# A decoder layer in fp32 on one core: other places for the matmuls that are issued as 64 and 192 columns

## The chip, the core and the metric

The kernel runs on one core of one Trainium2 chip, in one launch. The metric is the time of that core in device microseconds. All arithmetic is fp32; a matmul's operands are declared as fp32r.

## What is computed

One layer of a decoder trunk, batch 1, 256 tokens, model width 2048, cut here to its matrix products:

```python
n = rmsnorm(h, g_mix);  z = n @ w_in                  # 2048 -> 5120: q, k, v, u
a = moba_attention(q, k, v, dist_bias)                # 8 heads of 128, one block of 256 keys: causal
c = conformer_conv(u, conv_w, ...)                    # gated, 31 taps per channel, layernorm, silu
h = h + concat([a, c]) @ w_out                        # 2048 -> 2048
h = h + cross_attention(rmsnorm(h, g_cross), rmsnorm(mem, g_mem), wq, wk, wv, wo)   # 4 heads, 256 memory tokens
nm = rmsnorm(h, g_mlp)
h = h + square(relu(nm @ w1)) @ w2                    # 2048 -> 8192 -> 2048
return rmsnorm(h, g_final)
```

## The kernel before

**Steps.** The host lays all weights out as 200 chunks of 128 x 2048 elements (1 MB each), in the order of their use. The kernel is one straight program of 200 steps, step j for chunk j: u is steps 0 to 15 (U0), v 16 to 23 (V0), q and k 24 to 39 (QK0), the memory's k and v 40 to 47, w_out 48 to 63 (WOUT0), cross attention's wq and wo 64 to 71, and the MLP 72 to 199 (MLP0). The MLP has four rounds of 32 steps: 16 for a quarter of w1 (72 to 87, 104 to 119, 136 to 151, 168 to 183), then 16 for the same quarter of w2.

**Products.** The kernel splits each operand into a high part, rounded to fp32r, and a low part, the rest, and makes a product of three matmuls: high x high, high x low, low x high. SP loads chunk j into a `raw` tile (4 buffers), ACT rounds it to `wh` (`split_high`), DVE takes the difference `wl` (`split_low`; between steps 8 and 47 POOL does this for every seventh chunk); `wh` and `wl` have 3 buffers each and are made two steps ahead. Activations stand as `act`, `mixa`, `mixc` or `s` tiles, their high and low parts side by side.

**Two kinds of step.** In `weight_stationary` (u, q and k, the memory's k, w_out, w1) a 128 x 128 block of weights is loaded into TensorE and 256 columns of activations stream through it: 16 blocks of weights times three, so 48 products of 256 columns. In `act_stationary` (v, the memory's v, w2) activations are loaded and 512 columns of weights stream: 24 products of 512 columns. Each matmul has a weight load of its own, also where two matmuls in a row have the same weights. The number of a product in its step, 0 to 47, is called its place here: `3 * (4 * i + m) + n`, with i the slice of 128 rows of the chunk, m the block of 128 columns, and n which of the three (0 high x high, 1 high x low, 2 low x high).

**Issued in two.** The table `PARTED` (line 43) names steps and places; `weight_stationary` issues a product that stands in it as two matmuls on the same weights, the first of 64 columns, the second of the other 192:

```python
if 3 * (nf * i + m) + n in PARTED.get(j, ()):
    mm(bk, o[:, 0:64], a, b[:, 0:64], False)
    mm(bk, o[:, 64:], a, b[:, 64:], stop)
else:
    mm(bk, o, a, b, stop)
```

**What stands between the products.** The order of each engine's work is written out by hand: `at(place, j, fn, frac)` hangs work on a step (early, pre, late, mid, post), and mid hooks run between the units of a step, a unit being the 12 products of one i. On TensorE they are short: the sums for a norm (`totals`, in steps 5, 15, 48, 76, and after 64), its spread over the partitions (`spread`, two transposes, in steps 6, 16, 49, 77), the scores, transposes and values of self-attention (after step 28, in 30, in 31, and so on every four steps), cross attention in 65 to 71, and transposes of h inside some w2 steps. All else in a `weight_stationary` stretch is products of 256 columns, one after the other. DVE also has the 31 taps of the convolution, spread over steps 7 to 46 (`fill`).

Of the kernel before, what the change touches and what calls it, by code (L numbers as in the profile page):

```python
# [38 lines left out]
WOUT_ORDER = [(0, 0), (1, 0), (2, 0), (0, 1), (1, 1), (2, 1), (3, 0), (3, 1)]  # L39
STEP_US = 5.25  # L40


PARTED = {2: (3, 7, 11), 6: (24, 28, 32), 24: (3, 7, 11), 50: (3, 7, 11), 77: (24, 28, 32),
          104: (3, 7, 11), 136: (3, 7, 11), 168: (3, 7, 11)}
WARM = 14

ROOM = 128
# [35 lines left out]
def tile_hybrid_block(ctx: ExitStack, tc: tile.TileContext, xT, memT, w, par, rel, gfin, out):  # L83
# [21 lines left out]
    def mm(bk, o, lhsT, rhs, stop):  # L105
        pe.matmul(o, lhsT=lhsT, rhs=rhs, start=not bk.begun, stop=stop, skip_group_check=True)  # L106
        bk.begun = True
# [192 lines left out]
    def weight_stationary(j, banks, kg, acts, kts=4, cols=512, last=None):  # L300
        units = []
        nf = cols // P
        for i in range(kts):
            def unit(i=i):
                for m in range(nf):
# [5 lines left out]
                    for n, (a, b) in enumerate(((h, hi), (h, lo), (l, hi))):  # L311
                        stop = last and i == kts - 1 and n == 2
                        if 3 * (nf * i + m) + n in PARTED.get(j, ()):
                            mm(bk, o[:, 0:64], a, b[:, 0:64], False)
# [764 lines left out]
```

## Time and profile before

| | |
|---|---|
| runs of the kernel before | 1159.45 us median, 1157.51 to 1162.56, 3 runs |
| the profiled execution, its own time | 1160.12 us |
| its span, first to last instruction | 1158.3 us |
| TensorE clock granted over the span | 0.997 of full speed |
| matmuls in the program | 7978 |

The profile names engines PE (matmuls), PEld (weight loads, which run beside matmuls), DVE, ACT, POOL and SP. A row of the timeline has a start in us from the span's start, a length, and how many instructions in a row it merges (x). The length of a matmul's record is longer than the distance to the next start, since matmuls are pipelined; so paces are read here from starts, not from lengths. The trace holds starts to 1 ns, the views print them to 10 ns.

### The profile page before, as it was taken

Reading aid. Unit: us, or ns where it says so; the run is one execution under the profiler, and the core shown is the slowest. Engines: PE = TensorE matmul, PEld = TensorE weight load, DVE = VectorE, ACT = ScalarE, POOL = GpSimd, SP = SyncE. Lnnn points to the kernel's source line nnn. Section 1 sums busy time; section 2 is a strip of 40 time slices with the busy share of each in tenths; the row PEclk is TensorE's granted clock in tenths of the full one; section 3 lists DMA queues with packets and bytes.
Section 4 is the critical chain, followed back from the end, with each engine's and each line's share of the span. In section 5 each row is a group of like instructions: output and inputs, shape, how many; then the busy total and the mean of one; then the engine's idle time right before and its main releaser. Section 6 shows DMA issues by size and latency. Waiting matters only on the chain.

```text
span 1158.3 us, 18581 instructions
## 1 busy us (share of the span) xinstructions
PE 1144.4 (99%) x8038; PEld 1069.5 (92%) x8038; DVE 705.5 (61%) x821; ACT 540.3 (47%) x565; POOL 123.2 (11%) x104
## 2 busy tenths in 40 slices
PE   8999999999999999999999999999999999999997
PEld 8998899998999999998889998889999889999886
DVE  6699997878666768545444454554545554455443
ACT  7654335474655556444333444333454333444342
POOL 2282022102004003000000200000000000000112
PEclk9999999999999999999999999999999999999999
DMA  9874744455455535455555645555544555554541
GB/s 349 287 219 170 272 184 173 154 182 182 169 190 192 179 134 194 155 227 192 191 182 182 218 158 211 208 187 184 184 178 185 215 184 195 193 190 149 218 145 73
DMA packets 35289, 221.04 MB, mean 191 GB/s; under 512 B 3848, under 2 KB 7304, under 8 KB 9736
## 3 DMA queue, kind: packets, MB, share of 16 engines
q1 hardware_dynamic: 33024, 216.98, 51.7%
q10 hardware_dynamic: 2184, 2.88, 1.2%
q8 instruction: 63, 1.03, 0.4%
q14 instruction: 18, 0.15, 0.0%
HBM read 216.18 MB, written 3.67 MB: 190 GB/s over the span
## 4 chain that ended last, share of the span: by engine, by line
PE 92%; DVE 4%; ACT 1%; DMA 1%; issue 1%; ACTq 0%; POOL 0%; DVEq 0%
PE mm L106 86%; PE cv L106 3%; DVE cv L72 2%; DVE wl L72 2%; PE sm L106 2%; DMA raw<-in_w_dram 1%; ACT wh L172 0%; DMA hT<-in_xT_dram 0%; PE sm L840 0%; PE sm L525 0%; DVE small L72 0%; PE sm L715 0%; DVE ring L72 0%; ACT act L200 0%; POOL hp L420 0%
## 5 line engine op out<-in xcount | busy, mean ns | idle before, releaser
L72 DVE TENSOR_TENSOR wl<-raw,wh 128x2048 fp32r<-128x2048 f32 (+1 forms) x205 | 444.5, 2175 | 296.8 <-ACT wh L172 291.8
L172 ACT ACTIVATE wh<-raw 128x2048 fp32r<-128x2048 f32 x195 | 373.7, 1916 | 501.8 <-PE mm L106 448.2
L106 PE MATMUL mm<-act,wh 128*128 128x256 f32 (+1 forms) x3214 | 566.0, 280 | 1.3 <-ACT wh L358 1.3
L106 PEld LDWEIGHTS mm<-act,wh 128*128 128x128 f32 x3214 | 490.0, 188 | 2.2 <-ACT wh L358 1.6
L106 PE MATMUL mm<-act,wl 128*128 128x256 f32 x1607 | 447.0, 279 | 0.4 <-DVE wl L72 0.4
L106 PE MATMUL mm<-wh,s 128*128 128x512 f32 (+1 forms) x1040 | 319.1, 387 | 0.0
L106 PEld LDWEIGHTS mm<-act,wl 128*128 128x128 f32 x1607 | 301.2, 188 | 1.0 <-DVE wl L72 1.0
L106 PEld LDWEIGHTS mm<-wh,s 128*128 128x128 f32 x1040 | 194.3, 188 | 39.2
L106 PE MATMUL mm<-wl,s 128*128 128x512 f32 (+1 forms) x520 | 200.7, 386 | 0.0
L106 PEld LDWEIGHTS mm<-wl,s 128*128 128x128 f32 x520 | 97.7, 188 | 19.4
L72 DVE SCALAR_TENSOR_TENSOR cv<-hp,part,cv 128x256 f32<-128x256 f32 x240 | 97.6, 478 | 0.0
L72 DVE TENSOR_TENSOR s<-ring,s 128x512 fp32r<-128x512 f32 x32 | 22.2, 692 | 66.6 <-ACT s L828 66.6
L944 POOL TENSOR_TENSOR acc<-acc,gb 128x512 f32<-128x512 f32 x6 | 11.9, 2010 | 458.1 <-ACT ring L860 458.1
L106 PE MATMUL mm<-wh,act 128*128 128x512 f32 x192 | 60.1, 391 | 0.0
L225 POOL TENSOR_TENSOR acc<-acc,ring 128x512 f32<-128x512 f32 x17 | 39.9, 2344 | 147.0 <-ACT ring L224 146.3
L106 PE MATMUL mm<-mixa,wh 128*128 128x256 f32 (+1 forms) x258 | 45.6, 280 | 0.0
L106 PEld LDWEIGHTS mm<-wh,act 128*128 128x128 f32 x192 | 36.0, 188 | 7.4
L182 POOL TENSOR_TENSOR wl<-raw,wh 128x512 fp32r<-128x512 f32 x24 | 32.5, 1386 | 95.4 <-ACT wh L172 95.4
L106 PEld LDWEIGHTS mm<-mixa,wh 128*128 128x128 f32 x258 | 39.3, 188 | 0.2
L106 PE MATMUL mm<-wl,act 128*128 128x512 f32 x96 | 37.4, 389 | 0.0
L106 PE MATMUL mm<-mixa,wl 128*128 128x256 f32 (+1 forms) x129 | 35.7, 278 | 0.0
L106 PE MATMUL mm<-mixc,wh 128*128 128x256 f32 x192 | 32.7, 276 | 0.0
(141 smaller groups left out, 745.2 us busy)
## 6 DMA issues: line engine op xcount, KB each, us to landing
raw<-in_w_dram SPq DMA_DIRECT2D x199, 1024.0 KB, 4.8
mem<-in_memT_dram SPq DMA_DIRECT2D x4, 512.0 KB, 8.4
hT<-in_xT_dram SPq DMA_DIRECT2D x3, 512.0 KB, 8.5
dram_rev<-rev ACTq DMA_DIRECT2D x1, 1532.0 KB
raw<-in_w_dram SPq DMA_DIRECT2D x4, 256.0 KB, 5.7
bias<-dram_rev SPq DMA_DIRECT2D x1, 1024.0 KB, 8.2
gb<-in_gfin_dram SPq DMA_DIRECT2D x4, 256.0 KB, 7.4
out_dram<-acc SPq DMA_DIRECT2D x4, 256.0 KB, 2.7
```

Source lines behind the costliest of these rows:

```text
L72: return op(out, *args, **kw)
L106: pe.matmul(o, lhsT=lhsT, rhs=rhs, start=not bk.begun, stop=stop, skip_group_check=True)
L172: act.activation(wh[j], raw[j], AF.Copy)
L182: pool.tensor_sub(wl[j][:, s], raw[j][:, s], wh[j].bitcast(F32)[:, s])
L225: eng.tensor_tensor(self.acc, self.acc, sq, op=OP.add)
L944: pool.tensor_mul(d, d, gb[cb])
```

## The change

Only the table changes. Before, eight steps had three products each that were issued in two: at places 3, 7 and 11, or at 24, 28 and 32. Now nine steps have them: steps 2 and 72 three each, the other seven one each. That makes 13 in place of 24, so 11 matmuls fewer in the program. Step 72 is new in the table; step 2 is the first u stretch's, 72 is the first step of the MLP.

```diff
-PARTED = {2: (3, 7, 11), 6: (24, 28, 32), 24: (3, 7, 11), 50: (3, 7, 11), 77: (24, 28, 32),
-          104: (3, 7, 11), 136: (3, 7, 11), 168: (3, 7, 11)}
+PARTED = {2: (5, 20, 36), 6: (24,), 24: (5,), 50: (3,), 72: (6, 21, 37), 77: (24,), 104: (6,), 136: (6,), 168: (6,)}
```

The order of all other instructions, on PE and on the other engines, is the same; names below differ in running numbers alone, and lines by the two that the table got shorter.

On PE at the start of step 104 (an MLP stretch; steps 136 and 168 read alike), before: `wh104` and `wl104` are the high and low part of chunk 104, `act0` the activations, `mm` a PSUM bank.

```order
L106 MATMUL mm_275_6373<-act0_213_4730,wh104_6301 128x256 x2
L106 MATMUL mm_275_6373<-act0_213_4730,wl104_6302 128x256
L106 MATMUL mm_275_6373<-act0_213_4730,wh104_6301 128x64
L106 MATMUL mm_275_6373<-act0_213_4730,wh104_6301 128x192
L106 MATMUL mm_275_6373<-act0_213_4730,wh104_6301 128x256
L106 MATMUL mm_275_6373<-act0_213_4730,wl104_6302 128x256
L106 MATMUL mm_276_6374<-act0_213_4730,wh104_6301 128x256
L106 MATMUL mm_276_6374<-act0_213_4730,wh104_6301 128x64
```

And now, from the same point:

```order
L104 MATMUL mm_275_6368<-act0_213_4724,wh104_6296 128x256 x2
L104 MATMUL mm_275_6368<-act0_213_4724,wl104_6297 128x256
L104 MATMUL mm_275_6368<-act0_213_4724,wh104_6296 128x256 x2
L104 MATMUL mm_275_6368<-act0_213_4724,wl104_6297 128x256
L104 MATMUL mm_276_6369<-act0_213_4724,wh104_6296 128x64
L104 MATMUL mm_276_6369<-act0_213_4724,wh104_6296 128x192
L104 MATMUL mm_276_6369<-act0_213_4724,wh104_6296 128x256
L104 MATMUL mm_276_6369<-act0_213_4724,wl104_6297 128x256
```

The pair of 64 and 192 columns has moved from the fourth product (place 3) to the seventh (place 6, the first of the next block of weights), and the pairs at places 7 and 11 are gone.

On PE at the start of step 24 (the first of q and k), before:

```order
L106 MATMUL mm_56_1636<-act0_2_118,wh24_1533 128x256 x2
L106 MATMUL mm_56_1636<-act0_2_118,wl24_1534 128x256
L106 MATMUL mm_56_1636<-act0_2_118,wh24_1533 128x64
L106 MATMUL mm_56_1636<-act0_2_118,wh24_1533 128x192
L106 MATMUL mm_56_1636<-act0_2_118,wh24_1533 128x256
L106 MATMUL mm_56_1636<-act0_2_118,wl24_1534 128x256
L106 MATMUL mm_57_1637<-act0_2_118,wh24_1533 128x256
L106 MATMUL mm_57_1637<-act0_2_118,wh24_1533 128x64
```

And now:

```order
L104 MATMUL mm_56_1634<-act0_2_118,wh24_1531 128x256 x2
L104 MATMUL mm_56_1634<-act0_2_118,wl24_1532 128x256
L104 MATMUL mm_56_1634<-act0_2_118,wh24_1531 128x256 x2
L104 MATMUL mm_56_1634<-act0_2_118,wl24_1532 128x64
L104 MATMUL mm_56_1634<-act0_2_118,wl24_1532 128x192
L104 MATMUL mm_57_1635<-act0_2_118,wh24_1531 128x256 x2
L104 MATMUL mm_57_1635<-act0_2_118,wl24_1532 128x256
L104 MATMUL mm_57_1635<-act0_2_118,wh24_1531 128x256 x2
```

The pair stands at place 5, on the low weights, in place of 3, 7 and 11.

## Rows read from the trace of the kernel before

**Rows 1.** the page, part 1: busy us (share of the span), instructions of each engine.
```profile
PE 1144.4 (99%) x8038; PEld 1069.5 (92%) x8038; DVE 705.5 (61%) x821; ACT 540.3 (47%) x565; POOL 123.2 (11%) x104
```

**Rows 2.** what PE waited for, whole span: us in total, times, longest us.
```profile
PE sm L257 <- DVE rr L72: 1.9, 1, 1.9
```

**Rows 3.** sums by stretch of 20 us: busy time and matmuls touched (x), granted clock.
```profile
60.00:80.00 20.00, 20.00 (x179) 1.00 0.76 208
151.00:171.00 20.00, 20.00 (x173) 1.00 0.68 263
480.00:500.00 20.00, 20.00 (x179) 1.00 0.67 247
640.00:660.00 20.00, 20.00 (x172) 1.00 0.67 238
```

**Rows 4.** timeline of PE, first products of steps 78, 88, 104, 105, 120, 136 (start, length).
```profile
470.52 0.39 PE L106 MATMUL mm<-act,wh 128*128 128x256 f32 x2
...
524.92 0.39 PE L106 MATMUL mm<-wh,s 128*128 128x512 f32 x1
...
615.91 0.40 PE L106 MATMUL mm<-act,wh 128*128 128x256 f32 x2
...
621.88 0.28 PE L106 MATMUL mm<-act,wh 128*128 128x256 f32 x1
...
706.68 0.39 PE L106 MATMUL mm<-wh,s 128*128 128x512 f32 x1
...
793.75 0.40 PE L106 MATMUL mm<-act,wh 128*128 128x256 f32 x2
```

**Rows 5.** timeline of PE, step 50: first and third split product, and what follows each.
```profile
304.83 0.50 PE L106 MATMUL mm<-mixa,wh 128*128 128x64 f32 x3
305.17 0.28 PE L106 MATMUL mm<-mixa,wl 128*128 128x256 f32 x1
...
305.96 0.36 PE L106 MATMUL mm<-mixa,wl 128*128 128x64 f32 x2
...
306.42 0.28 PE L106 MATMUL mm<-mixa,wl 128*128 128x256 f32 x1
```

**Rows 6.** timeline of PE, first split product of steps 2, 6, 24 and 77.
```profile
20.43 0.50 PE L106 MATMUL mm<-act,wh 128*128 128x64 f32 x3
20.77 0.28 PE L106 MATMUL mm<-act,wl 128*128 128x256 f32 x1
...
46.52 0.50 PE L106 MATMUL mm<-act,wh 128*128 128x64 f32 x3
...
145.34 0.50 PE L106 MATMUL mm<-act,wh 128*128 128x64 f32 x3
145.68 0.28 PE L106 MATMUL mm<-act,wl 128*128 128x256 f32 x1
...
467.46 0.50 PE L106 MATMUL mm<-act,wh 128*128 128x64 f32 x3
```

**Rows 7.** timeline of PE, step 104: its fourth product is the first split one.
```profile
616.15 0.28 PE L106 MATMUL mm<-act,wl 128*128 128x256 f32 x1
616.27 0.50 PE L106 MATMUL mm<-act,wh 128*128 128x64 f32 x3
```

**Rows 8.** timeline of PE, first products of steps 29, 33, 37 and 41.
```profile
174.69 0.47 PE L106 MATMUL mm<-act,wh 128*128 128x256 f32 x1
...
200.58 0.47 PE L106 MATMUL mm<-act,wh 128*128 128x256 f32 x1
...
225.84 0.47 PE L106 MATMUL mm<-act,wh 128*128 128x256 f32 x1
...
251.10 0.47 PE L106 MATMUL mm<-act,wh 128*128 128x256 f32 x1
```

**Rows 9.** timeline of PE (step 16) and of DVE (step 8): a wait in each.
```profile
103.90 0.43 PE L257 MATMUL sm<-ident,rr 128*128 128x128 f32 x2 [1.88 <-DVE rr L72]
...
54.17 0.49 DVE L72 TENSOR_SCALAR cv<-hp,part 128x256 f32<-128x256 f32 x1 [5.14 <-POOL hp L420]
```

## The prediction

> **What bounds the kernel now.** I read the page first: PE is busy 99% of the span [rows 1]. Then what PE waited for: its longest wait is one of 1.9 us for DVE [rows 2]. So the end is set by how closely PE's own products follow each other, and a busy PE does not tell that. The third view is the sums by stretch. All four stretches run products of 256 columns at the granted clock 1.00 (2.4 GHz), but 20 us touch 179 of them in two stretches and 172 or 173 in the other two [rows 3]. First starts of steps give the paces: the 480 products of steps 78 to 87 take 524.92 - 470.52 = 54.40 us, 113.33 ns each (the **tight** pace); the 720 of steps 105 to 119 take 706.68 - 621.88 = 84.80 us, 117.78 ns each (the **wide** pace) [rows 4]. A step of 48 is 5.440 us tight and 5.653 us wide, 0.213 us apart, 4.44 ns a product. The 384 products of 512 columns in steps 120 to 135 take 793.75 - 706.68 = 87.07 us, 226.7 ns each, twice the tight pace; only products of 256 columns can gain. The wide pace holds in the three MLP stretches from 104, 136 and 168 (16 steps each), 24 to 32, 2 to 6, 70 to 77, and pieces behind pauses.
>
> **What decides the pace.** The two kinds of stretch have the same instructions, so something that lasts from product to product differs. Three products on the tight pace take 340.0 ns, which is 51 units of 6.667 ns (16 columns at 2.4 GHz); three on the wide one 353.3 ns, which is 53 units. I took starts in ns (the rows print 10 ns), averaged like products of a stretch, and read them against a grid of 6.667 ns, with a drift of 2 ns per ms taken out, to some 0.6 ns. In all the tight stretches of 256 columns the products begin at one and the same offset, also behind pauses; I call it 0. On the wide pace the products go round in threes, at offsets 1.7, 5.8 and 3.3 ns. So the two paces are two locks against a grid that outlasts pauses, and a split product knocks PE out of one. Where it then lands follows from the offset at which it begins. First splits of a step: in 6, 50 and 77 (at 46.52, 304.83 and 467.46) the offset is 1.7 ns, and the tight pace begins within two products, before the second split. In 2 and 24 (at 20.43 and 145.34) it is 5.8 ns, and the pace stays wide [rows 5, 6]. In 104, 136 and 168 it is 2 ns, but the round has not settled: the product ahead took 120 ns (616.27 - 616.15) [rows 7], and the pace stays wide. Second and third splits in those five steps begin from what the earlier ones left and tell nothing of a settled round.
>
> **The change part by part.** *Splits.* A split on the tight pace adds one tight product: from 305.96 to 306.42 three products, one of them split, take 0.46 us where three take 0.34 (113 ns in ns starts) [rows 5]. The winning one from the wide round takes with the product behind it 305.17 - 304.83 = 0.34 us (338 ns) in place of 0.236 [rows 5]; a losing one adds about 0.105 us (145.68 - 145.34 = 0.34) [rows 6]. The change has 11 fewer.
>
> *Places.* Which of the three products of a block is split does not matter in the trace: settled splits at 5.8 ns do the same on high x high as on low x high. Going on by threes: in step 24 place 3 is at 5.8 ns, 4 at 3.3, so the new place 5 is at 1.7; step 2 is alike. Step 72 stands in a settled wide round with place 0, and so 3 and 6, at 1.7. In 104, 136 and 168 place 3 is at about 2 ns behind the 120 ns product. Where a 120 ns product stands elsewhere (behind first or second splits in steps 2, 24, 104, 136, 168) the next takes 117 or 118 and begins the round; by that place 4 is at 5.8, 5 at 3.3 and 6 at 1.7. So all new places hit the winning offset. Steps 6 and 77 are entered otherwise than before, on the tight pace up to the norm's sums in 5 and 76. From the tight pace those sums left place 0 at 1.7 in steps 15 and 65, which is what step 77 had before; so place 24 wins in both as it did. Step 50 is untouched upstream.
>
> *The sum, against the run's own 1160.12 us.*
> MLP, each of three: before 706.68 - 615.91 = 90.77 us [rows 4]; after 6 wide products (0.71), the pair and its neighbour (0.338) and 760 at the tight pace (86.13), 87.18. 3 x 3.59 = **10.77**.
> Steps 24 to 32: step 24 had 48 wide products and three losing splits, 5.97; after 5 x 0.1178 + 0.338 + 41 x 0.1133 = 5.57: 0.40. Steps 25 to 28: 4 x 0.213 = 0.85. Steps 29 to 32 become like 37 to 40, which are entered tight: 200.58 - 174.69 = 25.89 us against 251.10 - 225.84 = 25.26 [rows 8]: 0.63. Together **1.88**.
> Steps 2 to 6: step 2 keeps three splits, two of them now on the tight pace: 5.97 to 5.80, 0.17; steps 3 and 4 0.43; step 5 up to its sums 36 x 4.44 ns = 0.16; step 6 loses two splits, 0.24. Together **1.00**. Step 16 takes some back: PE waits there 1.88 us for DVE [rows 9]. That DVE work goes back without a gap that matters to its wait at 54.17 for the first convolution input [rows 9], which stands behind step 6's spread. It moves by what is won ahead of that, 0.76, and the other 0.24 makes the wait longer: **-0.24**. Bounds: 0 if DVE keeps up, -1.00 if it does not move.
> Step 50: two splits fewer, **0.23**. Steps 72 to 77: step 72 gets three splits, -0.15; 73 to 75 0.64; 76 up to its sums 0.11; 77 two splits fewer, 0.23: **0.82**.
> Sum 14.46 us. PE's supply stands it: steps 7 to 14 and 78 to 87 run tight with no wait of PE. That gives 1145.7 by the run shown, which is 0.7 us over the median 1159.45: **1145.0 us**.
>
> **The rivals.** *1. The MLP places miss.* They are the one place where the round has to settle from products that no row shows without a split. If place 6 is not at 1.7 ns there, all three stay wide, since they are entered alike: 10.77 goes, two losing splits less each return 0.63, **1155.1**. For it: another entry of the kind "wide after a pause" (step 6, behind its spread) takes longer to settle than I assume here. Against: the five 120 ns products that can be read all went on into the round at once.
> *2. One smaller stretch misses.* Step 24 alone: 1.67 us, **1146.7**; step 77 or 50, which have no second try any more: 2.2 and 3.2, up to **1148.2**; one MLP stretch of three, 1148.4.
> *3. The place decides nothing.* The operands' addresses or the history set the pace, and only the splits saved count: 11 x 0.106 = 1.2, **1158.3**. The Trainium skill speaks for this kind of view ("TensorE: Matmul & The Clock Gate", "Step-by-step: what each phase is for"): weight loads and the streaming operand have separate read ports, and "Loading the next tile's weights doesn't steal SBUF read bandwidth from the running matmul", by which there should be one pace and no offset that matters. The trace does not agree: it has two paces at one clock [rows 3], and three times the pace changes behind a split.
> *4. Slower.* The single splits in 6, 50 and 77 lose, where three tries stood before, because the offset at a place is not carried over as I read it. Then 6 to 15, 50 to 64 and 77 to 87 turn wide: 432, 717 and 504 products x 4.44 ns = 7.3 us; with all new places missing too and 1.2 saved, **1165.6**. It decides as soon as two of the three old winners lose and no MLP stretch wins; one that wins (3.6) hides it. For it: before, runs differ by 5 us, about one MLP stretch and more, so offsets may differ between runs; the first steps wait for loads. Against: stretches 24, 104, 136 and 168 begin behind long rows of 512 columns that wait for nothing.
>
> **How the numbers follow.** Forecast 0.70 (1143 to 1147), rival 1 0.13, rival 2 0.09, rival 3 0.04, rival 4 0.04. A measurement of this kernel tells about 0.5% from no change, 5.8 us: faster is below 1153.7. Forecast and rival 2 are faster, 0.79; rivals 1 and 3 no change, 0.17; rival 4 slower, 0.04. The range reaches from 1142.5 (step 16 gives nothing back, and what runs differ by) to 1150 (one stretch misses and step 16 takes all back); it leaves out rivals 1, 3 and 4.
>
> **What would show it.** In the sums by stretch of the changed kernel 20 us anywhere in 105 to 119, 25 to 28 and 73 to 75 should touch 179 products, not 172. The stretch from step 104 to 120 should be 87.2 us long, and 29 to 33 25.3. PE's wait in step 16 should be 2.1 us. If the pace changes at a place whose offset is not 1.7 ns, or does not where it is, the grid is wrong; if the paces come as said and the time does not, the wait list has a new line.

## The result, and the profile after

The changed kernel takes 1146.78 us (median of 4 runs, 1145.39 to 1148.68) against 1160.03 us (median of 4 runs, 1157.51 to 1162.56): a ratio of 0.989 with a 95% interval of 0.987 to 0.991, so 1.1% faster and clear of no change. The forecast was 1145.0 us, between 1142.5 and 1150.0, faster with 0.79. Profile against profile the span went from 1158.3 to 1143.8 us, 14.5 us, where the sum had 14.46. That agreement is better than the reasons deserve: the big term came as worked out, and among the small ones 1.7 us were missed and 1.8 us came unforeseen (the table further below).

The page's part 1 of the kernel after (busy us, share of the span, instructions), to set beside [rows 1]:

```profile
span 1143.8 us, 18559 instructions
PE 1130.8 (99%) x8027; PEld 1056.0 (92%) x8027; DVE 705.6 (62%) x821; ACT 540.4 (47%) x565; POOL 127.3 (11%) x104
```

PE is as busy as it was, 99%. The share says nothing of the gain; busy time and span fell together. The sums by stretch of 20 us, to set beside [rows 3] (start:end, busy time and matmuls touched of PE, PEld, DVE, ACT, POOL, then granted clock, DMA share, GB/s):

```profile
60.00:80.00 20.00, 20.00 (x179) 20.00 (x178) 19.19 (x33) 11.04 (x12) 17.92 (x11) 1.00 0.75 216
151.00:171.00 20.00, 20.00 (x179) 20.00 (x178) 20.00 (x32) 6.34 (x4) 1.97 (x2) 1.00 0.69 263
480.00:500.00 20.00, 20.00 (x178) 20.00 (x178) 11.66 (x8) 8.04 (x8) 0.00 (x0) 1.00 0.58 207
640.00:660.00 20.00, 20.00 (x179) 20.00 (x178) 11.40 (x8) 8.40 (x6) 7.03 (x4) 1.00 0.76 264
```

151:171 and 640:660 had 173 and 172 products, now 179, at the same granted clock 1.00. These are steps 25 to 28 and 109 to 112. The timeline of PE, first products of steps 78, 88, 104, the split of 104 and the product behind it, and the first products of 105, 120 and 136, to set beside [rows 4, 7]:

```profile
466.80 0.39 PE L104 MATMUL mm<-act,wh 128*128 128x256 f32 x2
...
521.20 0.39 PE L104 MATMUL mm<-wh,s 128*128 128x512 f32 x1
...
612.21 0.40 PE L104 MATMUL mm<-act,wh 128*128 128x256 f32 x2
...
612.92 0.50 PE L104 MATMUL mm<-act,wh 128*128 128x64 f32 x3
613.26 0.28 PE L104 MATMUL mm<-act,wl 128*128 128x256 f32 x1
613.37 0.28 PE L104 MATMUL mm<-act,wh 128*128 128x256 f32 x1
...
617.79 0.28 PE L104 MATMUL mm<-act,wh 128*128 128x256 f32 x1
...
699.39 0.39 PE L104 MATMUL mm<-wh,s 128*128 128x512 f32 x1
...
786.46 0.28 PE L104 MATMUL mm<-act,wh 128*128 128x256 f32 x1
```

Steps 104 to 119 take 699.39 - 612.21 = 87.18 us, where they took 90.77, and 87.18 was the forecast. The pair and the product behind it take 613.26 - 612.92 = 0.34 us, the next start follows after 0.11 us (613.37): the tight pace from there on. Steps 105 to 119 are 699.39 - 617.79 = 81.60 us, 113.33 ns a product. 136 and 168 are equal to it.

The small stretches did not all come as said. PE in step 2, its first product, the first split, the third split with the product behind it, and the first product of step 3, to set beside [rows 6]:

```profile
20.02 0.40 PE L104 MATMUL mm<-act,wh 128*128 128x256 f32 x2
...
20.60 0.36 PE L104 MATMUL mm<-act,wl 128*128 128x64 f32 x2
...
24.47 0.50 PE L104 MATMUL mm<-act,wh 128*128 128x64 f32 x3
24.81 0.28 PE L104 MATMUL mm<-act,wl 128*128 128x256 f32 x1
...
25.99 0.28 PE L104 MATMUL mm<-act,wh 128*128 128x256 f32 x1
```

Step 2 took 25.99 - 20.02 = 5.97 us, as before: three losing splits, and steps 3 and 4 stayed at 5.653 us. The first products of steps 29, 33, 37 and 41, to set beside [rows 8]:

```profile
172.41 0.47 PE L104 MATMUL mm<-act,wh 128*128 128x256 f32 x1
...
197.98 0.58 PE L104 MATMUL mm<-act,wh 128*128 128x256 f32 x2
...
223.56 0.59 PE L104 MATMUL mm<-act,wh 128*128 128x256 f32 x2
...
249.13 0.47 PE L104 MATMUL mm<-act,wh 128*128 128x256 f32 x1
```

29 to 33 take 25.57 us (25.89 before, 25.26 forecast), and 33 to 41 take 51.15 where they took 50.52: steps 35 to 38 had been partly tight and are wide now.

What PE waited for in the kernel after (us in total, times, longest), to set beside [rows 2, 9]:

```profile
PE sm L148 <- POOL ident masks.py:199: 1.5, 1, 1.5
PE mm L104 <- ACT wh L356: 1.5, 1, 1.5
PE sm L255 <- DVE rr L70: 1.1, 1, 1.1
```

The last line is the wait in step 16: 1.1 us, not 2.1 as forecast.

### The profile page after: what moved, and what is told of

It reads as the page before. It is cut to its first block, busy times and chain, and to the rows that moved or that the text cites. A ratio compares the mean times of both kernels' runs of the same rounds, so it can differ in the third digit from the quotient of the medians.

```text
span 1143.8 us, 18559 instructions
## 1 busy us (share of the span) xinstructions
PE 1130.8 (99%) x8027; PEld 1056.0 (92%) x8027; DVE 705.6 (62%) x821; ACT 540.4 (47%) x565; POOL 127.3 (11%) x104
## 4 chain that ended last, share of the span: by engine, by line
PE 92%; DVE 4%; ACT 1%; DMA 1%; issue 1%; ACTq 0%; POOL 0%; DVEq 0%
PE mm L104 86%; PE cv L104 3%; DVE wl L70 2%; DVE cv L70 2%; PE sm L104 2%; DMA raw<-in_w_dram 1%; ACT wh L170 0%; DMA hT<-in_xT_dram 0%; PE sm L838 0%; DVE small L70 0%; PE sm L523 0%; PE sm L713 0%; DVE ring L70 0%; ACT act L198 0%; POOL hp L418 0%
## 5 line engine op out<-in xcount | busy, mean ns | idle before, releaser
L104 PE MATMUL mm<-act,wh 128*128 128x256 f32 x3209 | 553.6, 278 | 1.5 <-ACT wh L356 1.5
L104 PE MATMUL mm<-act,wl 128*128 128x256 f32 (+1 forms) x1603 | 443.8, 277 | 0.1
L104 PE MATMUL mm<-mixa,wh 128*128 128x256 f32 x257 | 45.0, 279 | 0.0
L104 PE MATMUL mm<-mixa,wl 128*128 128x256 f32 x128 | 35.4, 277 | 0.0
```

## Where the time went, stretch by stretch

The steps' lengths, from first start to first start, before minus after, beside the terms of the sum (us):

| stretch | forecast | measured |
|---|---|---|
| up to step 2 | 0 | 0.07 |
| steps 2 to 6 | 1.00 | 0.22 |
| step 16 | -0.24 | 0.75 |
| steps 24 to 38 | 1.88 | 0.93 |
| step 50 | 0.23 | 0.23 |
| steps 68 to 77 | 0.82 | 1.53 |
| three MLP stretches | 10.77 | 10.77 |
| sum | 14.46 | 14.50 |

All other steps together differ by 0.02 us, the other way.

Below, a round is named by the product of each triple of places that stands at the 1.7 ns offset: **first** (high x high as the code stands), **second** or **third**; **tight** is the tight pace. Both follow from starts in ns against the 6.667 ns grid, as in the prediction, with offset 0 taken from the tight stretches of the same trace. A split that is to turn the wide pace into the tight one is a **try**; it **wins** when the pace behind it is tight, and **loses** when it stays wide.

## Experiments

The edits are against the changed kernel. Runs of one kernel differ by 3 to 6 us, and e2 to e6 and e10 were run once each, so the readings rest on the lengths of steps, most of which repeat to 0.01 us.

**Run e1: no splits at all.** It asks what splits are worth, and whether the place is needed.

```diff
-PARTED = {2: (5, 20, 36), 6: (24,), 24: (5,), 50: (3,), 72: (6, 21, 37), 77: (24,), 104: (6,), 136: (6,), 168: (6,)}
+PARTED = {}
```

> All 13 splits are taken out, nothing else. My theory: nothing turns the wide pace any more. The stretch from step 104 to 120 takes 768 x 117.78 ns = 90.45 us in place of 87.2, the same for 136 and 168 (together +9.8 us); steps 24 to 28 are wide (+0.93), 51 to 64 too (+3.07), 78 to 87 too (+2.13), 6 to 15 too (+1.8, of which the 1.1 us that PE waits in step 16 swallow 1.1); the three losing splits of step 2 give 0.3 back and step 72 0.1 to 0.3. Sum +16 us: about 1163 us against 1146.8 for the changed kernel (1161 to 1165), so slower than the kernel before too. In 31 to 43 the pause rule that I now read in both traces must hold: a pause behind a wide round that has its 1.7 ns offset on the first product of each triple (high x high) ends tight, behind any other wide round it ends wide. Rival 3 of the prediction (place decides nothing, splits only cost): the paces stay as they are and 13 x 0.106 us go, 1145.4. A third view, that each stretch takes its pace from how it is entered and splits only follow it, has at least one of 51 to 64, 78 to 87 and 105 to 119 tight.

Measured: 1161.58 us, ratio to the kernel before 1.0018 (1.0006 to 1.0029), so no gain is left. The first products of steps 104 and 120:

```profile
617.83 0.28 PE L104 MATMUL mm<-act,wh 128*128 128x256 f32 x1
...
708.29 0.40 PE L104 MATMUL mm<-wh,s 128*128 128x512 f32 x1
```

90.46 us, and the same in 136 and 168; 7 to 14, 25 to 27, 51 to 63 and 78 to 87 all at 5.653 us. Rival 3 of the prediction (place decides nothing) would have had 1145.4 and falls; so does the view that entry alone sets the pace of these stretches. Steps 70 to 75 were tight without a split: these stand behind pauses (below).

**Run e2: other places.** By offset, 4 and 5 should lose in the MLP and 9 win.

```diff
-2: (5, 20, 36), ... 72: (6, 21, 37), ... 104: (6,), 136: (6,), 168: (6,)
+2: (5, 21, 37), ... 72: (), ... 104: (4,), 136: (5,), 168: (9,)
```

> The changed kernel, but step 104 has its split at place 4, 136 at place 5 and 168 at place 9 (all at 6 before); step 2 has 5, 21, 37 in place of 5, 20, 36, and step 72 has none. By offset, place 4 stands at 5.8 ns, 5 at 3.3 and 9 at 1.7: 104 to 119 and 136 to 151 stay wide (step 105 5.653 us; 90.55 us to step 120), 168 to 183 are tight from its place 10 on (87.2 us). In step 2 the three places are the third, first and second product of a triple, and a losing split leaves the offsets of the three kinds of product as they were, so one of the three must win whatever the start-up leaves: steps 3 and 4 take 5.440 us. Sum against 1146.8: +6.7 for two MLP stretches, -0.3 for step 72 if it is entered tight (+0.6 if wide), -0.2 to -0.8 for steps 2 to 5 as far as step 16 does not wait longer: about 1153 us. Rival (any single split turns a settled wide round): all three MLP stretches tight, 1146. Rival (a split wins only on a high x high product): the same as mine in the MLP stretches; e3 tells these two apart. For the losing splits the rival to my step 2 is that each leaves the round somewhere else: then 5, 21, 37 may lose as 5, 20, 36 did.

Measured: 1151.17 us. First products of steps 104 and 120, 136 and 152, 168 and 184:

```profile
610.95 0.40 PE L104 MATMUL mm<-act,wh 128*128 128x256 f32 x2
...
701.51 0.40 PE L104 MATMUL mm<-wh,s 128*128 128x512 f32 x1
...
788.59 0.40 PE L104 MATMUL mm<-act,wh 128*128 128x256 f32 x2
...
879.15 0.40 PE L104 MATMUL mm<-wh,s 128*128 128x512 f32 x1
...
966.23 0.40 PE L104 MATMUL mm<-act,wh 128*128 128x256 f32 x2
...
1053.43 0.39 PE L104 MATMUL mm<-wh,s 128*128 128x512 f32 x1
```

90.56, 90.56 and 87.20 us: as expected to 0.01. One place to the side costs a whole stretch, 3.4 us. In step 2 the round stood on the third product, and the first try, place 5, turned it (5.80 us, then 5.440).

**Run e3: other kinds of product at the same place.** In e2 the winners were high x high products; this run tells kind from offset.

```diff
-                    for n, (a, b) in enumerate(((h, hi), (h, lo), (l, hi))):
+                    three = ((h, hi), (h, lo), (l, hi))
+                    r = TURN.get(j, 0)          # TURN = {104: 1, 136: 2}
+                    for n, (a, b) in enumerate(three[r:] + three[:r]):
```

> The changed kernel, but the three products of every block come in another order in two stretches: in step 104 high x low, low x high, high x high; in step 136 low x high, high x high, high x low. Places and splits stay, so place 6 is now a high x low product in 104 and a low x high one in 136. If the offset decides, both win as before: 105 to 119 and 137 to 151 at 5.440 us, time as the changed kernel (1146.8, to within what runs differ by). If the kind of product or its operands' addresses decide, 104 and 136 stay wide: +6.7 us, 1153.5.

Measured: 1146.39 us. First products of steps 104 and 120:

```profile
612.97 0.28 PE L105 MATMUL mm<-act,wh 128*128 128x256 f32 x1
...
700.15 0.39 PE L105 MATMUL mm<-wh,s 128*128 128x512 f32 x1
```

104 to 120 and 136 to 152 take 87.18 us each, as 168 to 184 does. Place 6 wins as a high x low and as a low x high product. The kind of product and its operands do not decide.

**Runs e4 and e10: other sizes of the first piece.** All at the winning place 6.

```diff
-                            mm(bk, o[:, 0:64], a, b[:, 0:64], False)
-                            mm(bk, o[:, 64:], a, b[:, 64:], stop)
+                            f = FIRST.get(j, 64)   # e4: {104: 32, 136: 128, 168: 192}; e10: {104: 96, 136: 160, 168: 48}
+                            mm(bk, o[:, 0:f], a, b[:, 0:f], False)
+                            mm(bk, o[:, f:], a, b[:, f:], stop)
```

> The changed kernel, but the split at place 6 is cut as 32 + 224 columns in step 104, 128 + 128 in 136 and 192 + 64 in 168 (64 + 192 before). All are whole units of 16 columns, so by the offset alone each should win as 64 + 192 does, and the pair with the product behind it should cost about the same 338 ns, since in the trace the weight loads around a pair start 108 and 110 ns apart whatever the pieces are: 1146.8. Rival: what counts is when the second piece starts against its neighbours' weight loads; then at least one of the three sizes loses and its stretch stays wide (+3.4 us each, 1150 to 1157).

> More sizes of the first piece, at the winning place 6 of the changed kernel: 96 + 160 in step 104, 160 + 96 in step 136, 48 + 208 in step 168. So far 64 and 128 won, 32 and 192 lost; where it won, the pair and the product behind it took 338 ns, where it lost 340 (32) and 347 (192). Theory: the two that win bound a stretch of sizes in which the next weight load can follow at its own 108 to 110 ns; 96 wins (338 ns, step 105 5.440 us). For 48 and 160 the theory has no side: a loss of either narrows the stretch to 64 to 128 (3.4 us each), a win widens it. Time 1146 to 1153. Rival: the winning sizes are no stretch but multiples of 64 columns alone; then 96 loses too.

Measured: 1151.59 and 1145.39 us. In e4, first products of steps 104, 120, 168 and 184, and the 32 and 192 column pieces with the product behind each pair:

```profile
611.40 0.40 PE L105 MATMUL mm<-act,wh 128*128 128x256 f32 x2
...
612.11 0.50 PE L105 MATMUL mm<-act,wh 128*128 128x32 f32 x3
612.45 0.28 PE L105 MATMUL mm<-act,wl 128*128 128x256 f32 x1
...
701.96 0.39 PE L105 MATMUL mm<-wh,s 128*128 128x512 f32 x1
...
963.27 0.40 PE L105 MATMUL mm<-act,wh 128*128 128x256 f32 x2
...
963.98 0.51 PE L105 MATMUL mm<-act,wh 128*128 128x192 f32 x3
964.33 0.28 PE L105 MATMUL mm<-act,wl 128*128 128x256 f32 x1
...
1053.84 0.39 PE L105 MATMUL mm<-wh,s 128*128 128x512 f32 x1
```

90.56 us with 32 columns first, 90.57 with 192; 87.18 with 48, 64, 96, 128 and 160. So "multiples of 64" falls, and so does my expectation that all sizes win: the offset at which the split begins is needed, and is not enough. In starts in ns, the pair and the product behind it take 338 or 339 ns where it wins, 340 with 32 and 347 with 192. From an offset of 1.7 ns, 338 ns end at 339.7, within 0.3 ns of 51 units (340.0), where the tight products stand. That is an account of the winners, not proof: the split that loses from 5.8 ns takes 341 and ends at 346.8, as near to 52 units (346.7), and goes on wide. What tells these two apart is not in the starts. The two losing splits of e4 also moved the round, from the first product to the third.

**Run e5: several tries in one stretch.** Does a losing split leave the round on the same product?

```diff
-2: (5, 20, 36), ... 72: (6, 21, 37), ... 104: (6,), 136: (6,), 168: (6,)
+2: (5, 21, 37), ... 72: (6,), ... 104: (4, 20, 36), 136: (5, 21), 168: (4, 19)
```

> Several tries in one stretch, to see whether a losing split leaves the offsets of the three kinds of product where they were. Step 104: places 4, 20, 36; step 136: 5, 21; step 168: 4, 19; step 2: 5, 21, 37; step 72: 6 alone. In 104, 136 and 168 the 1.7 ns offset is on the first product of each triple (places 6 and 9 won, 4 and 5 lost). If losing splits keep it there: 104 loses at 4 (5.8 ns) and at 20 (3.3) and turns tight at 36, so step 104 is 5.93 us long and 105 5.440; 136 loses at 5 and turns at 21; 168 loses at 4 and 19 (both 5.8 ns) and stays wide to step 184 (90.66 us). Time against the changed kernel: +0.37, +0.2 and +3.5 us, less 0.2 to 0.9 in steps 2 to 5 and 72: about 1150.4 us. Rival (a losing split shifts the round): another of the tries wins, or none; most plainly 168 tight from 20 on, or 104 wide to its end. Rival of the pauses: after the self-attention pauses, a round on the second product goes to the third, on the third to the first, on the first to tight, in every case of steps 31 to 43; a different one ends that rule.

Measured: 1152.49 us. Step 104 was 5.93 us long and turned at 36, 136 turned at 21 (5.76 us), 168 stayed wide (90.67 us to step 184). All three as expected: a losing split of 64 and 192 columns keeps the round on its product, so tries must stand on different products of the triple. That is shown for tries 15 or 16 places apart; in the kernel before, three splits four places apart moved the round in steps 2 and 24 from the third product to the second. The time is 2.1 us over the expected 1150.4: behind a wait of 2.0 us in step 16 the granted clock was 0.50 (1.2 GHz) from 104.4 to 107.8 us, and that step took 9.54 us where e7's, with a wait of 1.9 us and the clock at 1.00, took 7.91. The changed kernel's 5, 20, 36 in step 2 are third, third and first, so a round on the second has no try at all. In the six traces with these places the round began step 2 on the second in three (none turned), on the first in two (turned at 36) and on the third in one (turned at 5). So the round that step 2 begins with differs from trace to trace.

**Run e6: fewer columns.** What is the tight pace made of?

```diff
-                            mm(bk, o, a, b, stop)
+                            w = COLS.get(j, T)   # 106, 138: 248; 107, 139: 240; 108, 140: 224; 109, 141: 192
+                            mm(bk, o[:, 0:w], a, b[:, 0:w], stop)
```

> What sets the tight pace itself. In eight MLP steps the products stream fewer columns (the rest of the result is left out there): 248, 240, 224 and 192 columns in steps 106 to 109, and the same in 138 to 141, all inside tight stretches. Theory A: the pace is the cycle from one weight load to the next (in both traces a load starts 3 ns behind the start of the product ahead, and the product 110 ns behind its load): then the starts stay 113.3 ns apart at 240 and 224 columns and the four steps stay 5.44 us long. Theory B: the pace is the columns' own time: 248 columns 109.8 ns, 240 106.3, 224 99.2, 192 85.0, so the four steps take 5.27, 5.10, 4.76 and 4.08 us. In between (A as a floor under B, for example the 108 ns at which loads stand closest around a split): 240 columns and fewer all take 108 to 110 ns, 5.2 us a step. Time of the kernel: 1146.8 by A, 1141.7 by B, about 1145 in between; steps 110 and 142 may enter wide (up to +2 us each), which would say that the lock needs 256 columns to hold.

Measured: 1151.29 us. First products of steps 106 to 111:

```profile
624.98 0.39 PE L105 MATMUL mm<-act,wh 128*128 128x248 f32 x2
...
630.42 0.27 PE L105 MATMUL mm<-act,wh 128*128 128x240 f32 x1
...
635.78 0.38 PE L105 MATMUL mm<-act,wh 128*128 128x224 f32 x2
...
641.13 0.38 PE L105 MATMUL mm<-act,wh 128*128 128x192 f32 x2
...
646.48 0.42 PE L105 MATMUL mm<-act,wh 128*128 128x256 f32 x2
...
652.16 0.28 PE L105 MATMUL mm<-act,wh 128*128 128x256 f32 x1
```

248 columns take 5.44 us a step as 256 do, 240 5.36, 224 5.35, 192 5.35; a quarter fewer columns save 1.7%. Theory B falls, and so does the sum of 5.2 us for the case in between; A is off by 1.5 to 1.7% from 240 columns down. From 248 to 192 columns the pace of these products is not their columns' time. Behind 192 columns the next step is wide (652.16 - 646.48 = 5.68), and the stretch stays wide to its end, which is the loss of up to 2 us a stretch that the expectation left open. In the starts of the kernel after, in ns, a weight load begins 3 ns behind the start of the product ahead, and the product 110 ns behind its load on the tight pace, 115 on the wide: the 4.4 ns lie between load and product. The Trainium skill names both instructions ("TensorE: Matmul & The Clock Gate", "Back-to-back issue gap"): in a stream of load and matmul pairs "the per-MM spacing is set by *both* ops". The runs agree in that fewer columns do not shorten the spacing in step with their number, and add that there are two spacings. The formula of the same section for an isolated matmul, N / 2.4 plus 2.5 ns, gives an estimate of 109.2 ns for 256 columns, which no stretch here reaches. What makes the two spacings, and what the grid of 6.667 ns is, no run here shows.

**Runs e7, e11 and e8: a better choice of tries, and the changed kernel again.** Four to six runs each.

```diff
-2: (5, 20, 36), ... 72: (6, 21, 37)
+2: (5, 21, 37), ... 72: (6,)
```

> The changed kernel with step 2 at 5, 21, 37 in place of 5, 20, 36 and step 72 at 6 alone in place of 6, 21, 37. Of step 2's three places the changed kernel had the third, third and first product of a triple; here it is each of the three once, so one must win. Step 72 is entered either tight, where each split costs 0.113 us, or wide with 1.7 ns on the first product, where 6 wins and the other two cost 0.226. My theory: 0.2 us less in step 72 in every run, and 0.6 us less in steps 2 to 5 in those runs whose start-up leaves the round on the second product (two of the four traces with 5, 20, 36 did not turn; with 5, 21, 37 all must). So 0.2 to 0.9 us under the changed kernel, 0.02 to 0.08%, which medians of runs may not tell apart; the trace must have steps 3 and 4 at 5.440 us. Rival: which round the start-up leaves is not what decides step 2, and 5, 21, 37 stays wide in some trace.

> The changed kernel again, unaltered, beside the candidate on the same chip: what differs from trace to trace. My theory: from step 78 on, in 6 to 15, 24 to 28 and 51 to 64 every step's time is the same to the ns as in the first trace; steps 0 to 5, 31 to 38 and 66 to 72 differ, by up to 0.7 us each way, because the pauses ahead of them wait for transfers and other engines and so end at another offset. Median 1146.8 (1145.4 to 1148.7). Rival 4 of the prediction, that the offsets of the long stretches differ between runs too: some MLP stretch wide, 3.6 us more.

> The kernel of run e7 once more, as the other side of e9 on one chip. 1144.9 us; PE's wait in step 16 1.0 us or more; step 2 turns at one of its three places whatever the start-up leaves (steps 3 and 4 5.440 us).

Measured: e7 1144.93 us (ratio to before 0.9879, 0.9860 to 0.9898), e11 1145.76 (0.9891, 0.9873 to 0.9910), and the changed kernel in e8 1145.70 (0.9883, 0.9862 to 0.9903). They can't be told apart by time. By steps, 72 is 0.23 us shorter in each (5.55 or 5.58 in place of 5.78 or 5.80). In the six traces with 5, 21, 37 step 2 turned at its first try in four (e7 among them) and was entered tight in two (e11 and e12), so the case that the new places are for, a round on the second product, did not come up; step 104 of e5 is that pattern, and won at its third try. In e8 every step of 24 to 28, 50 to 64 and 78 to 183 is as in the first trace to 2 ns (but for 20 ns in step 89), while steps 0 to 5, 16, 33 to 38 and 68 to 72 differ: 72 was entered wide, where the first trace had it tight.

**Runs e9 and e12: the wait in step 16.** The write of the distance bias, from a tile of its own, moved away, on top of e7; in one piece in e9, in four in e12.

```diff
-    at("early", 8, spread_bias)
-    at("early", 20, load_bias)
+    at("early", 18, spread_bias)      # e12: two heads each in 16, 18, 20, 22
+    at("early", 25, load_bias)        # e12: 24
```

> What PE's wait in step 16 hangs on. The kernel of run e7 (step 2 at 5, 21, 37; 72 at 6), with one more edit: the write of the distance bias to DRAM (1.5 MB in pieces under 2 KB, issued by ACT at 48.7 us in step 8) is issued in step 18, from a tile of its own, and the read back in step 25 in place of 20. My theory: this write crowds the weight chunks' transfers between 60 and 78 us (raw chunks there land after 9.6 to 11.0 us, 4.8 in the median of the whole run); one chunk comes late, ACT splits it late (at 75.1 to 76.5), DVE stands still for it for 0.8 to 1.6 us at 76 to 78 us, and its convolution and then the norm's chain of step 16 end that much later. Without the write DVE has no such gap, PE's wait in step 16 goes from 1.1 to 1.9 us to 0.3 or less, and the kernel gains 1.0 to 1.6 us on e7: about 1143.5. Rival: DVE has work enough without the gap (its chain is only shifted to the next wait): step 16's wait stays over 0.8 us and the time with it. Rival on the other side: the write crowds the chunks of steps 20 to 25 instead, PE waits for a weight tile there, 1 us or more slower.

> The kernel of run e9, but the bias write is issued in four parts of two heads each, in steps 16, 18, 20 and 22, and read back in step 24. In e9 PE's wait in step 16 was gone (0.2 us) but the write, in one piece, took 3.1 us from PE in step 25 and left 25 to 28 wide. If what hurts is its length in one stretch, the chunks between the parts catch up: no wait of PE in steps 17 to 25, step 25 5.440 us, 0.3 us or less in step 16: about 1144.2 us, 1 to 1.6 us under e7 and e11 (1144.9, 1145.8), which the medians may just tell. If the bytes have to be paid wherever they stand, the chunks run late through 18 to 25 all the same: PE waits 1 us or more there again, 1146 to 1149.

Measured: e9 1149.20 us beside e11's 1145.76, e12 1168.87. DVE's split of a weight chunk at 77 us in the kernel before, the kernel after, and e9 (in brackets its wait):

```profile
78.44 2.29 DVE L72 TENSOR_TENSOR wl<-raw,wh 128x2048 fp32r<-128x2048 f32 x1 [1.55 <-ACT wh L172]
```

```profile
77.41 2.29 DVE L70 TENSOR_TENSOR wl<-raw,wh 128x2048 fp32r<-128x2048 f32 x1 [0.81 <-ACT wh L170]
```

```profile
76.46 2.28 DVE L70 TENSOR_TENSOR wl<-raw,wh 128x2048 fp32r<-128x2048 f32 x1
```

And what PE waited for in e9:

```profile
PE mm L104 <- POOL wl L180: 2.5, 2, 1.4
...
PE mm L104 <- DVE wl L70: 1.3, 3, 1.0
...
PE sm L255 <- DVE rr L70: 0.2, 1, 0.2
```

Without the write DVE has no gap at 77 us and the wait in step 16 goes to 0.2 us (1.8 in e11, 1.9 in e7): the cause is as I had it for e9. The landings in the trace say the same: in the kernel before, the chunk issued at 57.57 us is all there at 76.38, and ACT splits it at 76.48; in e9 the one issued at 57.23 is there at 62.00. But the bytes are paid elsewhere. PE waits for weight tiles in steps 22 and 25, which are 6.69 and 8.63 us long in place of 5.44, and these pauses knock the tight pace out of 25 to 28. In four parts it is worse than either expectation: ACT's issues of the parts last 1.2, 1.5, 15.4 and 17.7 us, ACT splits chunks late behind them, and PE waits 15 us for weight tiles. Behind and between these waits the granted clock fell to 0.50 (1.2 GHz) in three stretches, 24 us together; products of 256 columns in step 24 stand 213 ns apart there. So the 23 us over e11 are waits and clock together. Two windows of PE in e12 (start:end, busy time and matmuls touched, granted clock, DMA share, GB/s):

```profile
135.00:140.00 5.00, 5.00 (x12) 0.50 0.65 207
185.00:190.00 5.00, 3.47 (x16) 0.50 1.01 418
```

No kernel here beats the changed one by an amount that can be measured.

## Why the forecast held, and where its steps failed

**MLP, 10.77: right in cause and size.** Place 6 wins, 4 and 5 lose, 9 wins (e2), whatever product stands there (e3), in all the traces alike (e8). Rival 1 fell with it, and rival 3 with e1. That the round there settles before place 6 was the open point, and it does. It has settled by place 3 already, which in the kernel after stands at 1.3 to 1.9 ns as place 6 does; yet the split at place 3 of the kernel before, which began at 1.4 to 2.1 ns, lost in all three stretches. The prediction put this down to the 120 ns product ahead of it. No run here splits place 3 alone, so that reason is not shown.

**Steps 24 to 28, 50, 6 and 77: right.** 1.25 of 1.25, 0.23, and the single splits turned the pace in 6 and 77. Rival 4 needed two of these to lose; none did in any of the twelve traces that have them.

**Step 2, 0.76 of the 1.00: failed.** The step was "step 2 is alike" (as step 24). I read where the round stands from one trace of the kernel before, third product, and took it over. It differs from trace to trace; here it stood on the second, and 5, 20, 36 have no try for that. That the waits of the start-up set it is likely and was not tested. Rival 4's argument named this ("the first steps wait for loads"), and I did not apply it to step 2.

**Steps 29 to 38, 0.95 of the 1.88: failed.** The step was "Steps 29 to 32 become like 37 to 40". 28, 29 and 30 did; then the pause in step 30 left the round on the third product, where in 38 it leaves it on the first. I had treated a pause as if it always ended alike. All 14 traces together give the rule for the pauses behind steps 28, 32, 36, 40 and in steps 31, 35, 39, 43:

| the round ahead of the pause | behind it | cases |
|---|---|---|
| first | tight | 44 of 44 |
| second | third | 15 of 15 |
| third | first | 16 of 16 |
| tight | tight | 37 of 37 |

So a wide round walks from second to third to first to tight over pauses and heals by itself, and steps 33 to 38 lose or gain by where the walk stands. The pauses in 30, 34, 38 and 42 have no such rule: they last 688 to 694 ns, and from tight they end on the first in 28 cases, the second in 10, the third in 2.

**Step 16, -0.24: wrong in sign.** The step was "without a gap that matters": DVE did stand still for 1.55 us at 77 us, for a chunk that lands late while the bias is written. After, that gap is 0.81 us, and it is this that shortened PE's wait from 1.88 to 1.1 us. It differs from run to run (e8 and e11 have gaps of 1.20 and 1.45 us, with waits of 1.5 and 1.8), so the 0.75 us are no merit of the change.

**Steps 68 to 77, 1.53 for 0.82: right in size from 72 on, for another reason.** The cross-attention pauses left PE tight from step 69 on, so 68 to 71 gained 0.69, and the three splits of 72, which were to turn the pace, only cost 0.13; 73 to 76 were tight without them. Of the 14 traces 7 enter step 72 tight and 7 wide on the first product, whatever stands in the table (e1 tight): not the change's doing either.

So 12.7 us of the 14.5 are the change, by offsets that the traces repeat (MLP 10.77, 24 to 28 1.25, and 0.23 each in 6, 50 and 77), and 1.8 are how the pauses and transfers of these two executions fell. The medians over runs, which average over such draws, differ by 13.3 us.

## What to carry to other kernels

When matmuls with a weight load each follow one another without a wait, read their pace from starts over tens of products, not from busy time, since two stretches of the same instructions at one granted clock can differ by 4%; a single matmul issued in two can move a stretch from one pace to the other, and where it stands decides. Trust such a place only where everything ahead of it runs without waiting; behind waits, spread the tries over all the states that the wait can leave. And a forecast that lands on the sum is to be read term by term before its reasons are believed.

## What was not expected of the hardware

- 256, 248, 240, 224 and 192 columns take 113.3, 113.3, 111.7, 111.5 and 111.4 ns each when every matmul has a load of 128 columns of weights (e6).
- What a pause does to the offset against a grid of 6.667 ns follows a rule without exception in 112 cases, although the pauses take 1.24 and 1.34 us from the last start ahead to the first behind.
- The same split turns the pace with 48, 64, 96, 128 or 160 of its 256 columns first and does not with 32 or 192 (e4, e10).
- Behind nearly the same wait in step 16, 2.0 and 1.9 us, the granted clock fell to 0.50 in e5, which cost that step 1.6 us, and stayed at 1.00 in e7.
- Beside a write of 1.5 MB in small pieces, the 1 MB transfers issued from 60 to 82 us land after 9.6 to 11.0 us in the median (kernels before and after; 4.8 over the whole run, 5.3 in the same window of e9, where the write stands later); cut into four it held up the engine that issued it for up to 17.7 us a part (e12).
